# Moving SyncE's wait for the last store behind the closing barriers

**Chip, cores, metric.** One core of one Trainium2 chip. The metric is device time in microseconds of one execution, the median of several. In the profiles SP is SyncE, ACT ScalarE, PE TensorE, POOL GpSimd and DVE VectorE (PEld is a part of PE); a `q` behind the name stands for the engine's sequencer, under which the profile lists the engine's waits, drains and semaphore updates. A semaphore is a counter that engines and transfers add to and that an engine can wait for; a barrier is a point that no engine passes before all have reached it.

## The reference

Max-unpooling with a factor of 2: each of 16·64·32·32 input values goes to one of four places of a 2×2 block, the other three are zero.

```python
out_i = i * kernel_size + idx // kernel_size
out_j = j * kernel_size + idx % kernel_size
output[b, c, out_i, out_j] = x[b, c, i, j]
```

`x` is 4 MB of float32, the indices are 8 MB of int64, the output is 16 MB.

## The kernel before

Three loads of 4 MB are issued ahead of the opening barrier: `x` by SyncE, two halves of the indices by ACT. VectorE makes four groups of output, each by four instructions `(index == place) * x`. SyncE stores each group when it is made, 4 MB a store, and then waits for all four stores:

```python
for g in range(NG):                                   # NG = 4
    nc.sync.wait_ge(made, g + 1)
    nc.sync.dma_start(out=out_v[g], in_=out_t[g]).then_inc(stored, 16)
nc.sync.sem_inc(made, -NG)
nc.sync.wait_ge(stored, 16 * NG).then_inc(stored, -16 * NG)
```

The framework puts two barriers behind this, in a block of its own. In the built program the block is, per engine (cut: one round is shown of two):

```
SP                    drain
PE, ACT, DVE, SP      drain, then gather += 1
POOL                  drain; wait gather >= 4, gather -= 4; release += 4
PE, ACT, DVE, SP      wait release >= 1, release -= 1
... (the same round once more)
```

## Time and profile before

| | us |
|---|---|
| median of the three first runs | 73.91 (73.86 to 73.93) |
| profiled run | 73.93 |
| span, from the program's first instruction to its last | 72.15 |
| VectorE's last instruction ends | 57.5 |
| the wait for the stores ends | 71.49 |

The lines of the profile are in the prediction below. How to read them: the page's busy slices and the windows say what is full (the DMA engines, nearly to the end), the waits of SyncE say what the program waits for last (the stores), and the view of one source line says when the instructions of the closing barriers ran. The views of the program end with the span. What the time holds beyond it is outside the program and shows only in the trace's records of semaphore updates.

### The profile page before, as it was taken

What the parts mean: (1) busy time and instruction counts of PE and PEld (TensorE: products, weight loads), DVE (VectorE), ACT (ScalarE), POOL (GpSimd) and SP (SyncE); (2) the same over time, 40 slices, a digit from 0 to 9 for tenths busy, and PEclk for the clock granted to TensorE, in tenths of its full rate; (3) what the DMA queues carried; (4) which work ended last, traced back from release to release, by engine and by line L of the source; (5) the groups of instructions that cost most, each with busy time, mean ns of one, the idle gap of its engine ahead of it and who ended that gap; (6) DMA issues with size and microseconds to landing.
All of it is one profiled execution on the core that took longest, in us unless ns stands there. A gap on an engine that the chain in (4) does not pass through costs nothing. (4 is left out here: it accounts for less than half of the span.)

```text
span 72.1 us, 67 instructions
## 1 busy us (share of the span) xinstructions
DVE 35.3 (49%) x16; POOL 0.2 (0%) x4
## 2 busy tenths in 40 slices
DVE  0000000000006999999999999999999900000000
POOL 1000000000000000000000000000000000000000
DMA  9689797979797979666969696969696979899990
GB/s 291 291 363 509 345 527 345 527 345 527 345 527 327 545 327 545 291 291 291 581 291 581 291 581 291 581 291 581 291 581 291 563 309 527 345 472 400 400 472 0
DMA packets 1008, 29.36 MB, mean 407 GB/s; under 512 B 112, under 2 KB 112, under 8 KB 112
## 3 DMA queue, kind: packets, MB, share of 16 engines
q1 hardware_dynamic: 720, 20.97, 68.6%
q10 hardware_dynamic: 288, 8.39, 26.9%
HBM read 12.58 MB, written 16.78 MB: 407 GB/s over the span
## 5 line engine op out<-in xcount | busy, mean ns | idle before, releaser
L123 DVE SCALAR_TENSOR_TENSOR out_t<-idx_t,x_t 128x2048 f32<-128x2048 int32 x12 | 26.5, 2289 | 22.2 <-DVEq L116 22.2
L123 DVE SCALAR_TENSOR_TENSOR idx_t<-idx_t,x_t 128x2048 f32<-128x2048 int32 x4 | 8.9, 2292 | 0.0
L154 POOL MEMSET const-bfloat16-1.0<- 128x1 bf16 x1 | 0.1, 101 | 0.0
L154 POOL MEMSET const-uint8-127<- 128x1 uint8 x1 | 0.1, 101 | 0.0
L154 POOL MEMSET const-float32-0.0<- 128x1 f32 x1 | 0.1, 98 | 0.2 <-issue 0.2
L154 POOL MEMSET const-float32-1.0<- 128x1 f32 x1 | 0.1, 98 | 0.0
## 6 DMA issues: line engine op xcount, KB each, us to landing
out_dram<-out_t SPq DMA_DIRECT2D x3, 4096.0 KB, 12.0
idx_t<-in_indices_dram ACTq DMA_DIRECT2D x2, 4096.0 KB, 26.5
x_t<-in_x_dram SPq DMA_DIRECT2D x1, 4096.0 KB, 21.9
out_dram<-idx_t SPq DMA_DIRECT2D x1, 4096.0 KB, 13.9
```

The source lines that it names most:

```text
L123: op = nc.vector.scalar_tensor_tensor(out=o_c[:, :, :, pidx // 2, :, pidx % 2], in0=idx_c[half][:, k : k + G], scalar=pidx, in1=x_c[:, G * ...
L154: nc = _bacc.Bacc("TRN2", target_bir_lowering=False, num_devices=1)
```

## The change

The wait is meant to stay in SyncE's program, so that the kernel still ends only after its last store, but to be its very last instruction, so that the two barriers run while the last store is still moving.

```diff
+    def last(self, made):
+        def move(nc):
+            ins = self.block.instructions
+            at = next(k for k, i in enumerate(ins) if i.name == made.ins.name)
+            nc.main_func.blocks[-1].instructions.append(ins.pop(at))
+        self.nc.at_finalize(move)
...
-        nc.sync.wait_ge(stored, 16 * NG).then_inc(stored, -16 * NG)
+        program.last(nc.sync.wait_ge(stored, 16 * NG).then_inc(stored, -16 * NG))
```

(Blank lines are cut.) Line numbers shift: the wait L137 is L147 in the changed kernel, and the barriers' L168 is L178.

## The prediction

> **What bounds the kernel now.** I read four views in this order: the page, to see which resource is full; the windows, to see whether it stays full to the end; SyncE's own waits, to see what the program waits for last; and the view of the source line that the closing barriers carry, to see what stands behind that wait.
>
> First the page. Lines from its head, busy slices and queues:
>
> ```profile
> span 72.1 us, 67 instructions
> DVE 35.3 (49%) x16; POOL 0.2 (0%) x4
> ...
> DMA  9689797979797979666969696969696979899990
> ...
> q1 hardware_dynamic: 720, 20.97, 68.6%
> q10 hardware_dynamic: 288, 8.39, 26.9%
> HBM read 12.58 MB, written 16.78 MB: 407 GB/s over the span
> ```
>
> VectorE works half of the span, the two DMA queues together 95.5% of it. The last digit of the DMA row is 0: the last slice (72.1 / 40 = 1.8 us) holds almost no transfer. The four windows below (load stage, VectorE stage, last store alone, closing) give VectorE busy, POOL busy, clock, DMA share and GB/s:
>
> ```profile
> 0.00:22.20 22.20, 0.00 (x0) 0.20 (x4) 1.00 0.97 404
> 22.20:57.60 35.40, 35.32 (x16) 0.00 (x0) 1.00 0.98 419
> 57.60:71.20 13.60, 0.00 (x0) 0.00 (x0) 1.00 0.95 407
> 71.20:72.15 0.95, 0.00 (x0) 0.00 (x0) 1.00 0.00 0
> ```
>
> So 29.36 MB at a full set of DMA engines sets the time up to 71.2 us, and no data moves after it. The chain of waits on the page ends with VectorE at 57.5 us, since it is followed back from the last engine instruction and leaves sequencers out; it says nothing of the last 14 us. SyncE's own waits do:
>
> ```profile
> SPq L137 <- SPq L137: 13.5, 1, 13.5
> SPq L168 <- PEq L168: 0.4, 2, 0.3
> ```
>
> L137 is the wait that the change moves: SyncE sits 13.5 us in it, until the 64th increment of the stores' semaphore. The view of L168, a line that only the closing barriers carry, has these rows (count, least/median/longest duration in ns, first and last start in us):
>
> ```profile
> L168 POOLq EVENT_SEMAPHORE  x4: 17/17/17, 71.6 to 72.0; - x4
> L168 SPq DRAIN  x3: 7/7/7, 71.5 to 71.8; - x3
> ...
> L168 DVEq DRAIN  x2: 19/8814/17608, 40.0 to 71.9; - x2
> L168 SPq EVENT_SEMAPHORE  x2: 17/17/17, 71.8 to 72.1; - x2
> L168 ACTq EVENT_SEMAPHORE  x2: 17/17/17, 71.8 to 72.1; - x2
> ...
> L168 PEldq EVENT_SEMAPHORE  x2: 51/51/51, 71.8 to 72.1; - x2
> ```
>
> The reader is to see that SyncE's three drains and two semaphore waits run one after another from 71.5 to 72.1 us, after L137, and that the waits of the other engines end with them: each barrier gathers four engines on POOL and releases them, and SyncE is the last to come to the first one. In the trace's records the wait L137 runs 71.471 to 71.488 us, SyncE's drains start at 71.550, 71.605 and 71.849, POOL's releases at 71.716 and 72.043, SyncE's last wait ends at 72.102 and PE's at 72.147, which is the span's end. So 72.147 - 71.488 = 0.66 us of the span is the two barriers behind the wait.
>
> The time is 73.91 us and the span 72.15, so 1.76 us more is counted outside the program. The trace keeps semaphore updates there, and these matter. One semaphore that no instruction of the program uses (number 2) gets nine increments at 72.38, 72.42, 72.62, 72.67, 72.69, 72.79, 72.83, 72.86 and 72.91 us; then five runs of about 50 resets each over all semaphores, from 72.81 to 73.47; then nine more increments of number 2, 73.69 to 74.05.
>
> [...] nine increments, most 20 to 50 ns apart, resets in runs of about 50, nine increments again. Going out and back through five engines gives nine updates, with the fifth as the turning point. Which engine that is I infer: the run of resets that starts first (semaphores 207 to 255, at 72.81) is the last fifth of the numbers and follows the fifth increment (72.69) by 0.12 us; the run that starts last (7 to 53, at 73.12, 8 ns each, the slowest) follows the ninth and belongs to the engine with the slowest sequencer, PE, as its 51 ns semaphore waits above show. PE first and SyncE fifth fits also the start of the program, where SyncE's first instruction is the first of all engines and PE's, at 0.31 us, the last. [...] L137 shows 17 ns for a wait of 13.5 us, and between SyncE's last drain of the first barrier and its release lie 71.757 - 71.605 = 0.15 us, of which the instructions shown fill 7 + 17 + 17 ns. The barriers' cost is therefore read from starts, not from durations.
>
> **The change part by part.** It moves one instruction of one engine. In the changed program SyncE issues the four stores, takes 4 off the count of VectorE's groups, branches, passes both barriers, and only then waits for the stores. Nothing is added or removed, and no transfer, VectorE instruction or order among them moves.
>
> Step 1, the last store's landing: unchanged. Loads start at 0, VectorE's last instruction ends at 57.55, the fourth store is issued at 57.575 and the semaphore is full at 71.45; the wait ends at 71.49 in both kernels.
>
> Step 2, the barriers: they go under the store. SyncE is free at 57.97, VectorE ends its drain at 57.59 and the others are waiting since 1.5 us, so both barriers, 0.61 us long for SyncE (72.102 - 71.488), run at about 58.0 to 58.6 us, beside a transfer that lasts to 71.2. All of the 0.61 us leaves SyncE's path. The span then ends with the wait itself: 71.49 to 71.51, 0.64 us less.
>
> Step 3, the runtime's first barrier: a further part may go. Before, PE's increment came 72.38 - 72.147 = 0.23 us after its last instruction, ACT's at most 72.42 - 72.106 = 0.31 us after, but the third, POOL's by my order, 72.62 - 72.06 = 0.56 us after. [...] SyncE's increment came 72.69 - 72.102 = 0.59 us after its own end though it may have been ready sooner. Now those four engines are through at 58.6 and their four increments are done by about 59.2; SyncE alone is awaited. If SyncE needs what PE and ACT needed, about 0.3 us, its increment comes at 71.505 + 0.30 = 71.8 instead of 72.69: 0.89 us earlier. If it needs the full 0.59 it saw before, it comes at 72.10: 0.60 us earlier. If it needs 0.2, 0.99 us.
>
> Step 4, everything after it (the way back, resets, second barrier): hangs on SyncE's increment and shifts by the same amount.
>
> Sum: 0.61 from the barriers, plus 0 to 0.38, taken as 0.25, from POOL's late arrival no longer being on the path: 0.86 us. 73.91 - 0.86 = 73.05 us, 1.2% less.
>
> **The rivals.** (A) Only the span shrinks: SyncE's own way into the runtime takes as long as POOL's, or the time outside the span is a constant 1.76 us. Then the gain is 0.60 to 0.64 and the time 73.27 to 73.31. What speaks for it is that nothing shows SyncE's own need directly; against it, that PE and ACT come in after 0.23 and 0.31. (B) Nothing is gained: the runtime has its own barrier and waits for SyncE anyway, so that the wait only takes another place, and 73.9 stays. Against it: the two kinds of barrier stand one after another, both before and outside the span in the trace, so removing the first from behind the wait shortens the row unless SyncE has a fixed later event to meet, and I see none. (C) The wait stops counting at all, the time ends with the other engines near 59 us, 12 us less. Against it: the wait is still in SyncE's stream and the runtime's barrier needs all five engines. (D) Slower: four engines enter the runtime's closing code 12 us early and disturb the store. Against it: before, too, they only waited in this stretch; [...] the resets in the trace come after the barrier's turn, so none can touch the stores' semaphore before the wait has ended. I give this 1%.
>
> **Range and chances.** The part that is sure is 0.60; the upper end adds the whole of step 3. 73.91 - 0.60 = 73.31 and 73.91 - 0.99 = 72.92, with the three runs before spread over 0.07 us; I take 72.85 to 73.35. A change over 2% needs 1.48 us, as much as nearly the whole stretch outside the span; so within 2% has 0.96, faster 0.03, slower 0.01.
>
> **What would show it.** Step 1: the stores' semaphore full at 71.4 to 71.5 us and the DMA share of each window as above. Step 2: the rows of barriers at 58 to 59 us in place of 71.5 to 72.1, the wait as the last instruction, and a span of 71.5 us. Step 3: the third increment of number 2 near 59.2 and the fifth some 0.2 to 0.6 us after the wait; the time minus the span then falls from 1.76 to about 1.5. A time of 73.3 with the span at 71.5 says that step 3 failed and (A) holds; a span of 71.5 with 73.9 says (B). A fifth increment that is not SyncE's would make the order I inferred wrong. A landing that moves by more than 0.1 us would mean the transfers were not left alone, and the whole sum would have to be drawn anew.

## The result, and the profile after

| | median us | range, runs |
|---|---|---|
| before | 73.87 | 73.84 to 73.93, 5 |
| changed | 72.77 | 72.68 to 72.88, 5 |

The ratio is 0.9852, 95% interval 0.9838 to 0.9865. It is the mean time of one kernel's fast runs over that of the other's of the same rounds, so not quite the ratio of the medians. The gain is 1.10 us where 0.86 was predicted, and 72.77 lies 0.08 under the stated range.

The page of the changed kernel, span, busy slices and queues:

```profile
span 71.4 us, 67 instructions
DVE 35.3 (49%) x16; POOL 0.2 (0%) x4
...
DMA  9789696969697989866979969696969696979985
...
q1 hardware_dynamic: 720, 20.97, 69.2%
q10 hardware_dynamic: 288, 8.39, 27.2%
```

The same instructions and bytes. The last digit of the DMA row is 5 where it was 0, but that is no sign of the change by itself. These views count a packet whole in the slice in which it starts. In both kernels the last 16 large packets start at 69.7 to 69.9 us and end by 71.1; with the shorter span the last slice starts at 69.66 us instead of 70.34 and so holds some of them. The same four windows (VectorE busy, POOL busy, clock, DMA share, GB/s):

```profile
0.00:22.20 22.20, 0.03 (x1) 0.20 (x4) 1.00 0.96 401
22.20:57.60 35.40, 35.29 (x16) 0.00 (x0) 1.00 0.99 426
57.60:71.20 13.60, 0.00 (x0) 0.00 (x0) 1.00 0.92 395
71.20:71.45 0.25, 0.00 (x0) 0.00 (x0) 1.00 0.00 0
```

Up to 71.2 us little has moved: VectorE's last end, the issue of the last store and its landing come 0.04 to 0.06 us earlier. A packet is counted in the window in which it starts, so a few around 57.6 change sides (0.98 and 0.95 become 0.99 and 0.92). The last window is the change: 0.95 us have become 0.25. SyncE's own waits and the view of the barriers' line in the changed kernel:

```profile
SPq L147 <- SPq L147: 12.9, 1, 12.9
```

```profile
L178 POOLq EVENT_SEMAPHORE  x4: 17/17/17, 58.1 to 58.5; - x4
L178 SPq DRAIN  x3: 7/7/65, 58.0 to 58.3; - x3
...
L178 SPq EVENT_SEMAPHORE  x2: 17/17/17, 58.2 to 58.6; - x2
L178 ACTq EVENT_SEMAPHORE  x2: 17/17/17, 58.2 to 58.6; - x2
```

The reader is to see that both barriers now run from 58.0 to 58.6 us, under the last store, and that the wait is shorter by just that (13.5 to 12.9 us) and ends within 0.04 us of the same time.

What follows the program, from the trace's semaphore records. No instruction of the program uses semaphore 2. The nine increments that it gets behind the program's barriers are called the runtime's first closing barrier here, and the nine after them the second; from the fifth increment on, five runs of resets of other semaphores start. The nine are read as a turn that passes through the five engines and back. For increments 1 to 5 the engine names follow the order that the prediction inferred and runs 6 to 9 confirm. The way back is inferred from the resets: in both traces one run of them starts after each of increments 5 to 9, 0.11 to 0.22 us later:

```
                         before                    changed
stores' semaphore full   71.455                    71.415
SyncE's last instr ends  72.102                    71.449
PE    increment 1        72.382                    58.870
ACT   increment 2        72.416                    58.904
POOL  increment 3        72.621                    59.109
VectE increment 4        72.666                    59.153
SyncE increment 5        72.689  (0.587 after)     71.583  (0.134 after)
VectE increment 6        72.787                    71.627
...   increment 9        72.907                    71.747
second barrier, incr. 6  73.933                    72.773
time of this run         73.93                     72.77
```

By this table the 1.16 us between the two profiled runs divide without a rest. The wait ends 0.04 earlier (71.488 to 71.449). The barriers on SyncE's path fall away, 0.614 (72.102 - 71.488). From SyncE's last instruction to its increment there are 0.587 - 0.134 = 0.453 less. From there to the end there are 0.054 less (1.244 to 1.190). Why 0.587 became 0.134 is what the experiments ask.

### The profile page after: what moved, and what is told of

The parts are those of the page before. It is cut to its first block, busy times and chain, and to the rows that moved or that the text cites. A ratio compares the mean times of both kernels' runs of the same rounds, so it can differ in the third digit from the quotient of the medians.

```text
span 71.4 us, 67 instructions
## 1 busy us (share of the span) xinstructions
DVE 35.3 (49%) x16; POOL 0.2 (0%) x4
```

## The experiments

Theory T: POOL increments 0.56 us after its last instruction and thereby holds the runtime's barrier up, while SyncE itself needs only 0.13. Rivals: R1, SyncE itself needs 0.59 when it comes out of a barrier and 0.13 only when a wait is its last instruction; R3, it is enough to stand behind the first barrier; R4, an engine needs little only where it has waited long; R5, some slack is left in the changed kernel. Medians are set beside the kernel before of the same chip: 73.89 us for runs 1 to 4, 73.87 for runs 5 to 8, 73.94 for runs 9 to 12, which ran on another chip. All twelve returned the right result. "Need" is the time from an engine's last instruction's end to its increment of semaphore 2, from the trace.

**1. The wait between the two barriers.**

```diff
-            nc.main_func.blocks[-1].instructions.append(ins.pop(at))
+            ...
+            end.insert(waits[0] + 1, ins.pop(at))
```

(Cut: the lines that set `end`, the closing block, and `waits`, the places of SyncE's barrier waits in it.)

> SyncE's wait stands between the two closing barriers. Theory T (POOL holds up the runtime's barrier, 0.56 us after its own last instruction; SyncE itself needs only 0.13 us): one barrier of some 0.33 us goes under the store, the other stays behind the wait, and POOL leaves it as late as before, so only about 0.33 of the 1.1 us is gained: 73.5 us, fifth increment of the runtime's semaphore still 0.55 to 0.6 us after SyncE's last instruction. Rival R1 (SyncE itself needs 0.59 us when it comes out of a barrier and 0.13 when it comes out of a wait at its end): also 73.5, so this run does not tell T from R1. Rival R3 (it is enough that the wait stands behind the first barrier): 72.8.

Measured 73.50 us (73.42 to 73.65), ratio 0.9949 (0.9933 to 0.9965). The barriers' line in this kernel:

```profile
L185 POOLq EVENT_SEMAPHORE  x4: 17/17/17, 58.1 to 71.5; - x4
L185 SPq DRAIN  x3: 7/7/71, 57.9 to 71.4; - x3
...
L185 SPq EVENT_SEMAPHORE  x2: 17/17/17, 58.2 to 71.6; - x2
```

One barrier runs at 58, the other at 71.4 to 71.6, behind the wait. POOL's last instruction ends at 71.542 and its increment comes at 72.103, 0.561 later, as before the change; SyncE's comes 0.586 after its own end. R3 falls. The single barrier is worth 0.39 us here (0.33 was expected; in the traces SyncE's stretch from the wait's end to its last instruction shrinks by just that, from 0.614 us to 71.584 - 71.358 = 0.226). The last one is worth 0.7 more: it is dear because POOL leaves through it.

**2. The wait in its old place, the barriers deleted.**

```diff
+    def no_barriers(self):
+        def cut(nc):
+            del nc.main_func.blocks[-1].instructions[1:]
+        self.nc.at_finalize(cut)
...
+        program.no_barriers()
```

> The wait is where it was before; both closing barriers are deleted from all engines (one drain of SyncE stays behind the wait). T: what counts is only that no barrier and no late POOL stands behind the wait; the drain costs some 0.06 us: 72.8 us, within 0.1 of the changed kernel. R1 (the wait must be the last of the stream): SyncE's need returns to up to 0.59 us, 73.3 us.

Measured 72.86 us (72.77 to 72.92), ratio 0.9859 (0.9841 to 0.9877), correct. SyncE's waits in this run still show the full wait, now with no barrier line behind it:

```profile
SPq L143 <- SPq L143: 13.5, 1, 13.5
...
SPq L161 <- PEq L161: 0.8, 1, 0.8
```

(L161 is the opening barrier.) SyncE's increment comes 0.19 us after the wait's end, its one drain included, and 0.12 us after that drain. So the gain does not come from the wait being last. It comes from no barrier, with POOL's way out, standing behind it. R1 predicted 73.3 and falls. Deleting does no better than moving.

**3 and 4. Four semaphore instructions more on SyncE, and on POOL, in the kernel before.**

```diff
+        for k in range(4):
+            program.last(nc.sync.sem_inc(pad, 1 - 2 * (k % 2)))    # run 4: nc.gpsimd
```

(The wait is in its old place.)

> The kernel before, with four semaphore instructions of SyncE (up, down, up, down on a spare semaphore) behind the last barrier, 0.04 to 0.08 us each, 0.16 to 0.32 in all. T: SyncE is ready 0.46 us before POOL has passed the turn on, so they are free: 73.87 within noise, fifth increment unmoved at 0.62 us after the release of the last barrier. R1: SyncE is the one that is late, so all of it is added: 74.05 to 74.2.

Measured 73.83 us (73.76 to 73.94), ratio 0.9994 (0.9977 to 1.0011). SyncE ends at 72.230, 0.19 us after PE, and still increments 23 ns after VectorE: free.

> The kernel before, with the same four semaphore instructions on POOL behind its last barrier instruction. T: [...] all of it is added: 0.16 to 0.32 us, 74.05 to 74.2. R1: POOL is not on the path, 73.87 within noise.

Measured 74.21 us (74.11 to 74.33), ratio 1.0043 (1.0027 to 1.0059). POOL's four:

```profile
L150 POOLq EVENT_SEMAPHORE  x4: 17/17/17, 72.2 to 72.4; - x4
```

They are 78.5 ns apart, 0.314 us in all. The median grows by 0.32, and POOL's increment stays 0.562 behind its last instruction. POOL is on the path of the kernel before and SyncE is not; this pair is the plainest evidence against R1.

**5. Sixteen on SyncE in the kernel before.** The edit is that of run 3 with `range(16)`.

> The kernel before with sixteen of SyncE's semaphore instructions behind the last barrier (58.7 ns each by the run with four: 0.94 us). Theory T (SyncE always needs some 0.13 us from its last instruction to its increment): it passes its 0.46 us of slack and comes in 0.13 us after its last instruction, so the time grows by 0.43 to 0.48 us: 74.3 to 74.35. Rival R4 (0.13 holds only where SyncE had long been waiting and its next instructions were at hand; on the run it needs as much as PE's 0.235 or more, up to 0.59): 74.4 to 74.8, the increment 0.24 us or more after its last instruction.

Measured 74.32 us (74.27 to 74.41), ratio 1.0055 (1.0034 to 1.0076).

```profile
L150 SPq EVENT_SEMAPHORE  x16: 17/17/17, 72.2 to 73.1; - x16
```

SyncE's last instruction ends at 73.094 and its increment comes at 73.223: 0.129 us, on the run and straight out of sixteen instructions. R4 falls for SyncE. Of the 0.94 us added, 0.45 show, so about 0.49 was slack.

**6 to 9. The wait as the last instruction of another engine.**

```diff
-        program.last(nc.sync.wait_ge(stored, 16 * NG).then_inc(stored, -16 * NG))
+        program.last(nc.gpsimd.wait_ge(stored, 16 * NG).then_inc(stored, -16 * NG))
         # run 7: nc.tensor, run 8: nc.scalar, run 9: nc.vector
```

> The wait for the stores is the last instruction of POOL instead of SyncE. T (what an engine needs is its own and does not shrink by waiting; POOL 0.56 us, then two hops of 0.04 and 0.02 to SyncE, and 0.05 more on the way back as DVE has just sent its own): POOL's increment 0.56 after the wait, 73.3 us. R4 (an engine that waited long needs 0.13): POOL's increment 0.13 after the wait, 72.9 us.

Measured 73.28 us (73.27 to 73.44), ratio 0.9921 (0.9902 to 0.994). POOL's increment comes 0.561 us after the wait: 13 us of waiting did not shorten it, and R4 falls for POOL too.

> The wait is the last instruction of PE. T: PE needs its 0.235 us, then four hops of about 0.04 to SyncE, which comes in some 0.28 us later than in the changed kernel: 73.05 to 73.15 us. R4: PE needs 0.13, 72.95 to 73.0 us.

Measured 73.19 us (73.11 to 73.20), ratio 0.9902 (0.9884 to 0.992), a little above the 73.05 to 73.15 of T: PE needed 0.278 us here, not 0.235. Why the two differ was not tried.

> The wait is the last instruction of ACT. ACT's own need was never seen free: 0.31 us at most, since its increment always followed PE's by 0.034. T with 0.31: 73.1 us; if ACT needs no more than SyncE's 0.13: 72.9 us.

Measured 72.95 us (72.91 to 73.15), ratio 0.9877 (0.9857 to 0.9897). ACT needs 0.144 us. The 0.31 that the kernel before showed was PE's lateness and a hop.

> The wait is the last instruction of VectorE. VectorE's own need was never seen free (0.549 us in every run, but it always followed POOL's increment by 0.044). If it is like SyncE's and ACT's (0.13 to 0.14): SyncE's increment 0.02 later than VectorE's, and 0.05 more on the way back: 72.85 us. If 0.5: 73.25 us.

Measured 72.90 us (72.77 to 73.05), ratio 0.9859 (0.9846 to 0.9873). VectorE needs 0.182 us, close to the low case and far from 0.549. (The expectation overlooked run 2, where 0.549 does not hold: without barriers VectorE's increment came at 57.557, 0.146 us after its last instruction, long after POOL's at 1.867.) In the four runs the engines named before the one that waits have their increments at 58.7 to 59.0 us and those behind it follow the wait. That is what proves the order PE, ACT, POOL, VectorE, SyncE:

```
semaphore 2, increments 1 to 5 (us)
wait on POOL    58.806  58.840  71.957  72.001  72.024
wait on PE      71.817  71.851  71.889  71.934  71.957
wait on ACT     58.841  71.590  71.629  71.672  71.695
wait on VectorE 58.734  58.768  58.973  71.498  71.522
```

**10 to 12. The changed kernel again, and with more instructions on SyncE (four, behind the wait) and POOL (sixteen).** The edits are the loop of run 3, in the changed kernel.

> The changed kernel itself, beside the other runs of this group: 72.77 us, ratio 0.985, SyncE's increment 0.13 us after the wait.

Measured 72.73 us (72.71 to 72.89), ratio 0.984 (0.9827 to 0.9853); increment 0.134 us after the wait.

> The changed kernel with SyncE's four semaphore instructions (58.7 ns each) behind the wait. Theory T (behind the moved wait SyncE alone sets the end, no slack is left): all of the 0.235 us is added, where the same four were free in the kernel before: 73.0 us. Rival R5 (another engine still gives some slack behind the wait): less than half of it, under 72.9.

Measured 73.07 us (73.00 to 73.15), ratio 0.9882 (0.9868 to 0.9895): 0.34 us over the changed kernel of the same group by the medians. In the two profiled runs SyncE's increment moves from 71.608 to 71.847, 0.24 as expected; the rest is within the spread of 0.15 to 0.18 us of each kernel's runs. R5 falls: SyncE now has no slack.

> The changed kernel with sixteen of POOL's semaphore instructions (78.5 ns each, 1.26 us) behind its last barrier instruction. T: POOL is done 12 us before the wait ends, so all of it is free: 72.77 us, where four of them cost 0.33 in the kernel before. R5: slower by up to 1.3 us.

Measured 72.82 us (72.72 to 72.85), ratio 0.9845 (0.9832 to 0.9859). POOL's last instruction ends at 59.84 instead of 58.58, and SyncE's increment still comes 0.134 after its wait. The 1.26 us are free where 0.31 cost its full length before.

No experiment beat the changed kernel.

## Why the prediction was wrong, point by point

- **Step 1 (the landing is unchanged) held.** The stores' semaphore is full at 71.415 instead of 71.455 us.
- **Step 2 (0.61 us of barriers go under the store) held:** no barrier stands behind the wait any more, both run at 58.0 to 58.6 us as forecast, and the span is 0.70 us shorter, of which 0.04 is the earlier landing, where 0.64 was said.
- **Step 3 failed in one term, not in its mechanism.** It said rightly that POOL's late arrival holds SyncE up and would drop off the path; runs 3, 4 and 12 show this. It mis-sized SyncE's own need: "If SyncE needs what PE and ACT needed, about 0.3 us", with 0.2 as the lowest case. It is 0.134. The saving of this term is therefore 0.587 - 0.134 = 0.45 us, not the 0.25 that was taken, and also more than the 0.38 that was the most allowed. Two slips stand behind it. ACT's 0.31 was read as a duration though it was only a bound: ACT's increment came 0.034 behind PE's, in its turn, and run 8 shows 0.144. And PE's 0.235 was carried over to SyncE though the prediction itself had called PE's sequencer the slowest (51 ns for a semaphore wait, where the others show 17 to 21).
- **The sum was then shaded.** Step 3 worked out 0.89 and a span of 0.60 to 0.99, and the sum took 0.86. With the measured 0.134 the same sum gives 0.61 + 0.45 = 1.06, or 72.85 us; with the 0.05 of step 4 below it gives 1.11, where 1.10 was measured.
- **Step 4 (all behind SyncE's increment shifts rigidly) held but for 0.05 us.** VectorE's answer to SyncE takes 0.098 us where VectorE has sent its own increment 0.023 us before, and 0.044 where it has waited (before against changed; likewise in runs 6, 7, 8 and 9 against run 5). The prediction had the first number in its trace and no case of the second.
- **The rivals:** (A) would have been 73.3, (B) 73.9, (C) some 60, (D) over 73.9; none came. What (D) feared did not happen: in the changed kernel the first reset comes at 71.704 us, after the wait's end at 71.449. The chance of 0.96 for a change within 2% fits the measured 1.5%. The mark set for step 3, the time less the span going from 1.76 to about 1.5 us, went further: 1.32.
- **Readings that were loose, without effect on the sum.** The 0 at the end of the DMA row was read as a last slice with almost no transfer; it comes from counting packets where they start, and the last packet ends at 71.11 us, well inside that slice. The chain of waits does not leave sequencers out, it lists DVEq L168; it ends at 57.5 because it starts from the last instruction of an engine that is not its sequencer's. And rival (C)'s 59 us and its "12 us less" do not agree.

What stays open: why POOL takes 0.56 us from its last instruction to its increment. Neither waiting (run 6) nor more work ahead of it (run 4) changes it, and no run took it apart.

## What to carry to other kernels

In this kernel, the only one tried, it paid to put the wait for the last store behind everything that does not need its result, so that barriers and the other engines' way out run under the transfer: it gained 1.1 us of 73.9. The engine mattered too: on SyncE, VectorE or ACT, which left 0.13 to 0.18 us after the wait, it gave 72.7 to 73.0 us; on PE and POOL, which left 0.28 and 0.56 us after it, 73.2 to 73.3. An early place in the runtime's order cost the hops to SyncE on top: 0.105 us from ACT's increment to SyncE's in run 8 (71.590 to 71.695), 0.140 from PE's in run 7 (71.817 to 71.957). And when a gap is read from a trace, ask whether it is a duration or only a bound: an engine that follows another in its turn shows nothing of what it needs itself.

## What else the traces show of the closing

- The engines enter the runtime's closing barrier at different delays. From the last instruction to the increment there are 0.56 us for POOL (the kernel before, runs 1, 4 and 6), 0.235 (before, changed) to 0.278 (run 7) for PE, 0.146 (run 2) to 0.182 (run 9) for VectorE, 0.144 (run 8) for ACT, and 0.12 (run 2) to 0.134 (changed) for SyncE.
- Runs 6 to 9 show the order PE, ACT, POOL, VectorE, SyncE; the way back is inferred, as said above. The mean hop is (74.052 - 73.695) / 8 = 0.045 us in the second closing barrier before. In the two traces, before and changed, hops to an engine that is not late are 0.023 us (VectorE to SyncE) to 0.048 (ACT to PE on the way back), but 0.098 for SyncE to VectorE where VectorE has just sent its own.
- In the kernel before, the run of resets that is put down to SyncE (semaphores 207 to 255) takes 0.08 us and the one put down to PE (7 to 53) 0.35, and from the end of the first barrier to the start of the second there are 0.79 us.
- In both traces the reported time falls within 0.01 us of the sixth increment of the second closing barrier, counted from SyncE's first instruction: 73.93 for 73.933 before, 72.77 for 72.773 changed. So a part of the runtime's closing code seems to be in the metric, 1.78 us behind the span before and 1.32 after.
- The place of the wait for the last store: between the two barriers it gave 73.50 us, behind both 72.73 to 72.77, ahead of both 73.87.
